# First weight sums formed in the HGRN2 stage, mixer splits one tile ahead, and a new order of the down projection's snapshots and splits

## The chip, the cores and the metric

The kernel runs on one core of one Trainium2 chip. The metric is the device time of one execution in microseconds. The kernel before has a median of 1284.31 us over three runs (1282.35 to 1285.01).

## The reference

One decoder layer for 1024 tokens of width 1024, all in fp32:

```python
u = rmsnorm(h, attn_pre_norm)
xp = u @ w_in                                  # MLA latents, rotary key, HGRN2 q, f, i, g
mix = concat(mla_mixer(...), hgrn2_mixer(...)) # 8 attention heads, 4 recurrence heads
h = h + rmsnorm(mix @ w_out, attn_post_norm)
z = rmsnorm(h, ffn_pre_norm)
ff = silu(z @ w_gate) * (z @ w_up)             # width 2816
h = h + rmsnorm(ff @ w_down, ffn_post_norm)
```

## The kernel before

Every fp32 matrix product is done as three TensorE products of values that are split in a high part (a cast on ScalarE, ACT) and a low part (a subtraction, mostly on VectorE, DVE). So each 128-row operand costs one cast and one subtraction before TensorE (PE) can use it.

The stages in order of time: the input norm with the first projection; HGRN2, a loop over four heads (L391), each with its projections and a chain of levels between PE, DVE, ACT and GpSimd (POOL); the latent projection; attention; the mixer, that is the output projection over eight row tiles of 128 tokens (L1137 to L1176) with the post norm (`post_y`, `post_z`) and the transposes into the FFN's operands (`z_t`); gate and up; down.

Both FFN matmuls use a scheme with seven products of half-size blocks in place of eight (Strassen's, in Winograd's form). It needs sums of weight blocks. For most of gate and up they are formed in the loop by DVE (`w_sums`, L1022). For the first four (block `m` = 0 to 3) `w_pre` (L1004) forms them during the mixer: two loads of 512 KB, four sums of 128x512 on POOL, two stores to the DRAM buffer `ws_d`, from where `w_load` (L996) fetches them later. Its two tiles come from the ring `wr` of two buffers (L103), which also serves the raw rows of `split`, the early weights (`w_early`, L1018) and the last row tile's input (`x_get(last)`, L927).

The mixer's tile `t` is split by `mix_load` (L826) into tiles of tags `mh` and `ml`, two buffers each; a whole tile needs both. `mix_load(t)` stands just before `mix_mm(t)` (L839), behind the norm work of tile `t - 1`. Up to L1148 a planner orders each engine's instructions by their place in the program (earlier goes first) and by when it reckons them ready, so the written place is a priority and not the final order. From L1148 on the order on each engine is the written one. Each engine runs its queue in order: an instruction that waits holds all behind it.

The down projection (L1399 to L1419) runs 77 steps: seven products of 11 steps, in the order p1, p2, p6, p5, p3, p7, p4. `d_load(n)` (L1272) fetches 512 KB for step `n` into one of four raw slots, `d_prep(n)` (L1277) splits it, five steps ahead of use, into one of eight split buffers, `d_mm(n, j)` runs its products for row block `j`. At the end of a product the last three steps (eight for p4) run block by block, and `d_post(p, j)` (L1363) reads block `j`'s result from PSUM: a copy or a sum ("snapshot"). p2 goes on accumulating in p1's banks, p3 in p5's, p7 in p6's, so that their first matmul of a block waits for that block's snapshot. p4 takes the banks that p7 has left.

Of the kernel before, what the change touches and what calls it, by code (L numbers as in the profile page):

```python
# [21 lines left out]
P = 128  # L22
S = 1024
D = 1024
# [64 lines left out]
def hymba_block(ctx: ExitStack, tc: tile.TileContext, a: dict, out: bass.AP):  # L89
# [287 lines left out]
    def chunk(x, c):  # L377
        return x[:, c * P:(c + 1) * P]

    tails = []  # L380

    def tail():
# [8 lines left out]
    for h in range(HH):  # L391
# [97 lines left out]
        for g in range(2):  # L489
            ops = sm(f"ho{h}_{g}").rearrange("p (c t) -> p c t", t=P)  # L490
            on = hp.tile([P, 4, P], F32, name=f"on{h}_{g}", tag="kn", bufs=3)
            for j in range(4):
                c = 4 * g + j
                T.matmul(ops[:, j, :], chunk(at, c), hv[:, c, h * P:(h + 1) * P], start=True, stop=(c == 0))
                if c > 0:
                    T.matmul(ops[:, j, :], chunk(q, c), st[:, c - 1, :], start=False, stop=True)
            i0 = h * NT + 4 * g
            for j in range(4):
                A.activation(on[:, j, :], ops[:, j, :], AF.Square, accum_out=ssh[:, i0 + j:i0 + j + 1])
            rsqrt(inh[:, i0:i0 + 4], ssh[:, i0:i0 + 4], 4, f"h{h}_{g}", 1.0 / P)  # L500
            for j in range(4):
                A.activation(on[:, j, :], ops[:, j, :], AF.Copy, scale=inh[:, i0 + j:i0 + j + 1])
            tails.append((h, g, on, sg))

    ssl = cst.tile([P, NT, 2], F32, name="ssl")
    inl = cst.tile([P, NT, 2], F32, name="inl")
# [319 lines left out]
    def mix_load(t, ks, mpool, tag, bufs):  # L826
        ts_ = slice(t * P, (t + 1) * P)
        for i in range(0, len(ks), 4):
            kn = ks[i:i + 4]
            k0, n = kn[0], len(kn)  # L830
            src = (mixb if k0 >= 4 else mixa)[:, k0 % 4:k0 % 4 + n, ts_]
            mh, ml = (mpool.tile([P, 4, P], F32R, name=f"m{x_}{t}_{k0}", tag=f"{tag}{x_}", bufs=bufs)[:, 0:n, :]
                      for x_ in "hl")
            A.copy(mh, src)
            V.tensor_tensor(ml, src, f32(mh), op=ALU.subtract)
            for j, k in enumerate(kn):
                mx_[t, k] = (mh[:, j, :], ml[:, j, :])

    def mix_mm(t, ks, ds=(0, 1)):  # L839
        if t not in yp_:  # L840
            if t not in Y_SMALL:
                y = big(f"y{t}")
                yp_[t] = [y[:, d_] for d_ in halves]
            else:
                yp_[t] = [sm(f"y{t}_{d}") for d in range(2)]
        for k, d in [(k, d) for k in ks for d in ds]:
            d_ = halves[d]
            mm3(yp_[t][d], mx_[t, k][0], mx_[t, k][1], wo[k][0][:, d_], wo[k][1][:, d_], k == order[0], k == order[-1])
# [138 lines left out]
            z_t2(t, tp)  # L987
            z_split("b22", tp[1], zc(t))

    w_of = {0: a["w_gate"], 1: a["w_up"]}  # L990
    seq = [(0, "p1"), (1, "p1"), (0, "p2"), (2, "p1"), (1, "p2"), (2, "p2"), (3, "p1"), (0, "p6"), (3, "p2"), (1, "p6")]
    seq += [(m, p) for p in ("p5", "p7", "p3", "p4") for m in range(2)]
    seq += [(m, p) for m in range(2, 2 * NP) for p in PRODUCTS if m > 3 or p not in ("p1", "p2")]
# [2 lines left out]
    def w_load(m):  # L996
# [3 lines left out]
        if m < PRE:  # L1000
            SP.dma_start(ffq["s1", m % 2], w_of[m % 2][m // 2 + NP][:, 512:1024])
        ws_[m] = wq.rearrange("p j (k c) -> p (j k) c", c=512)

    def w_pre(m):  # L1004
        pre_ = [wr.tile([P, D], F32, name=f"wp{m}_{j}", tag="wr") for j in range(2)]
        for j in range(2):
            SP.dma_start(pre_[j], w_of[m % 2][m // 2 + NP * j])
        (a11, a12), (a21, a22) = ([x_[:, d_] for d_ in halves] for x_ in pre_)
        G.tensor_tensor(a22, a21, a22, op=ALU.add)
        G.tensor_tensor(a21, a11, a21, op=ALU.subtract)  # L1010
        G.tensor_tensor(a11, a22, a11, op=ALU.subtract)
        G.tensor_tensor(a12, a12, a11, op=ALU.subtract)
        for j in range(2):
            SP.dma_start(ws_d[m, j], pre_[j])

    early = {}

# [110 lines left out]
    SP.dma_start(apost, a["attn_post"].partition_broadcast(P))  # L1128
    SP.dma_start(fpre, a["ffn_pre"].partition_broadcast(P))
    for t in range(NT - 1):  # L1130
        if t < 2:
            mix_load(t, order[6:8], cp, "m", 2)
            mix_mm(t, order[6:8])
        else:
            mix_load(t, order, cp, "m", 2)
            mix_mm(t, order)
        if t == 1:  # L1137
            finish_t(HEADS // 2 - 1, (1,))
        if t >= Z_LAG:
            z_t(t - Z_LAG, sm)  # L1140
        post_y(t)
        post_z(t)
        if t < PRE:
            w_pre(t)

    last = NT - 1
    mix_load(last, order, cp, "m", 2)
    ms = tc.manual_schedule(engines=None)  # L1148
    ms.__enter__()
    for x_ in "ab":  # L1150
# [121 lines left out]
    def d_load(n):  # L1272
        p, i = steps[n]
        SP.dma_start(dgen[:, n % 4, 0:512], fa_d[p][i])
        SP.dma_start(dgen[:, n % 4, 512:1024], b_src[p](i))
# [49 lines left out]
    def d_hl(n):  # L1325
        return dhp.tile([P, 2, 1024], F32R, name=f"dhl{n}", tag="dhl", bufs=8)
# [36 lines left out]
    def d_post(p, j):  # L1363
        o = dq[dbank[p]][j]
        p1, u2, u3, p5 = (x_[:, j, :] for x_ in (p1_, u2_, u3_, p5_))
        if p == "p1":
            A.copy(p1, o)  # L1367
        elif p == "p2":
            half(j, 0, o, True)
        elif p == "p6":  # L1370
            V.tensor_tensor(u2, o, p1, op=ALU.add)
        elif p == "p5":
            A.copy(p5, o)
        elif p == "p3":
            V.tensor_tensor(u2, o, u2, op=ALU.add)
            todo.append(lambda: half(j, 1, u2, False))
            todo.append(lambda: out_t(j, (0, 1), False))
        elif p == "p7":
            V.tensor_tensor(u3, o, p1, op=ALU.add)

            def c22():
                V.tensor_tensor(p5, p5, u3, op=ALU.add)
                half(4 + j, 1, p5, True)
            todo.append(c22)
        elif p == "p4":
            V.tensor_tensor(u3, o, u3, op=ALU.add)
            half(4 + j, 0, u3, False)
            out_t(4 + j, (1, 0), j == 3)
# [10 lines left out]
    for n, (p, i) in enumerate(steps):  # L1399
        if n + DN_AHEAD < len(steps):  # L1400
            if n + DN_AHEAD >= DN_EARLY + 4:
                d_load(n + DN_AHEAD)
            d_prep(n + DN_AHEAD, d_hl(n + DN_AHEAD))
        if i == 0 and p not in ("p2", "p7", "p3"):
            dq[dbank[p]] = [psd.tile([P, 512], F32, name=f"dy_{dbank[p]}{j}", tag="dy", bufs=8) for j in range(4)]
        if (p, i) in (("p4", 0), ("p3", 0)):
            for j in range(4):
                h1_load(4 * (p == "p4") + j)
        if todo and (i % 2 == 0 if p == DN_PRODUCTS[-1] else i < 8):
            todo.pop(0)()  # L1410
        tail_n = DN_END if p == DN_PRODUCTS[-1] else DN_LAST
        if i < NP - tail_n:
            for j in range(4):
                d_mm(n, j)
        elif i == NP - 1:
            for j in range(4):
                for x_ in range(n - tail_n + 1, n + 1):
                    d_mm(x_, j)
                d_post(p, j)  # L1419
    ms.__exit__(None, None, None)  # L1420
    d_st.close()
    w4_st.close()
# [87 lines left out]
```

## Time and profile before

The profiled execution took 1285.21 us; its span, from the first to the last instruction, is 1283.4 us, so 1.8 us lie around it. It is 0.9 us above the median of the three timed runs.

| engine | busy us | share of the span |
|---|---|---|
| PE (matmul) | 1230.8 | 96% |
| PEld (weight load) | 1024.2 | 80% |
| DVE | 905.6 | 71% |
| ACT | 560.4 | 44% |
| POOL | 328.5 | 26% |

A row of the timeline is start, duration, engine, line, operation, output <- inputs, shapes, count; in square brackets how long the engine had been idle just before, and what ended that. The DMA queue of the SP engine is SPq. Windows give the busy time of each engine in a stretch.

### The profile page before, as it was taken

The numbers are of one execution on the slowest core, as the hardware profiler recorded it, in microseconds if no ns is written. First come the engines' busy times: TensorE is split into PE (matmuls) and PEld (weight loads), VectorE is DVE, ScalarE is ACT, GpSimd is POOL, SyncE is SP. The second block draws the span as 40 slices with busy tenths as digits, with TensorE's granted clock in tenths as the row PEclk, the third lists the DMA queues.
The fourth block names the chain that finished last, engine by engine and source line by source line (L and its number), as shares of the span: only waits on it lengthen the run. The fifth ranks groups of instructions, "written<-read, shape, count | busy, mean of one in ns | idle before, by whom it ended". The sixth has DMA issues, their size and how long they took to land.

```text
span 1283.4 us, 18152 instructions
## 1 busy us (share of the span) xinstructions
PE 1230.8 (96%) x6436; PEld 1024.2 (80%) x6436; DVE 905.6 (71%) x1790; ACT 560.4 (44%) x1206; POOL 328.5 (26%) x395
## 2 busy tenths in 40 slices
PE   7999999999899998999999999999999998999997
PEld 6987777899788877777777888888888876888885
DVE  6836666552888889686987777767777865554586
ACT  6434343435867667443543232233232233444442
POOL 1015434321132334133003243323233432000010
PEclk8999999999999999999999999999999999999998
DMA  7240100102000002465524435444435558657691
GB/s 276 103 131 18 50 14 23 36 1 69 13 14 7 21 14 62 136 213 201 194 82 156 168 144 189 158 154 146 170 128 189 188 186 281 213 180 250 209 311 66
DMA packets 64554, 165.69 MB, mean 129 GB/s; under 512 B 7504, under 2 KB 8912, under 8 KB 64464
## 3 DMA queue, kind: packets, MB, share of 16 engines
q1 hardware_dynamic: 63360, 160.87, 36.5%
q0 software_dynamic: 1104, 3.67, 0.9%
q8 instruction: 51, 0.84, 0.3%
q14 instruction: 39, 0.32, 0.1%
HBM read 119.16 MB, written 45.35 MB: 128 GB/s over the span
## 4 chain that ended last, share of the span: by engine, by line
PE 69%; DVE 13%; DMA 6%; ACT 5%; issue 3%; POOL 3%; SPq 0%; DVEq 0%; ACTq 0%; POOLq 0%
PE g_B L1065 9%; PE g_E L1065 8%; PE g_A L1065 8%; PE dy_B L1396 5%; PE dy_E L1396 5%; PE g_C L1065 4%; PE dy_A L1396 2%; PE ao L772 2%; PE lv L441 2%; PE dy_C L1396 1%; DVE s L741 1%; PE lat_ps L99 1%; PE lat_ps L97 1%; PE lat_ps L98 1%; DMA w<-in_w_down_dram 1%
## 5 line engine op out<-in xcount | busy, mean ns | idle before, releaser
L1280 DVE TENSOR_TENSOR dhl<-w,dhl 128x1024 fp32r<-128x1024 f32 x74 | 92.3, 1267 | 65.0 <-ACT dhl L1279 64.7
L1279 ACT CAST dhl<-w 128x1024 fp32r<-128x1024 f32 x74 | 76.2, 1048 | 100.7 <-DMA w<-in_w_down_dram 29.7
L1046 ACT CAST wva<-w 128x512 fp32r<-128x512 f32 x62 | 37.8, 617 | 92.6 <-DVE w L1027 41.3
L1047 DVE TENSOR_TENSOR wva<-w,wva 128x512 fp32r<-128x512 f32 x62 | 55.5, 895 | 31.5 <-ACT wva L1046 31.3
L1046 ACT CAST wvb<-w 128x512 fp32r<-128x512 f32 x62 | 37.5, 616 | 90.4 <-DVE w L1027 49.7
L1047 DVE TENSOR_TENSOR wvb<-w,wvb 128x512 fp32r<-128x512 f32 x62 | 52.2, 843 | 32.9 <-ACT wvb L1046 32.8
L1119 POOL TENSOR_TENSOR wdr<-wdr 128x512 f32<-128x512 f32 x11 | 16.4, 1488 | 198.2 <-DMA wdr<-in_w_down_dram 184.7
L742 ACT ACTIVATE pe<-s,nm 128x128 f32<-128x128 f32 (+3 forms) x64 | 47.7, 746 | 40.3 <-DVE nm L741 24.5
L1396 PE MATMUL dy_B<-dhl 128*128 128x512 f32 x264 | 60.2, 389 | 0.0
L1396 PE MATMUL dy_E<-dhl 128*128 128x512 f32 x264 | 60.0, 389 | 0.0
L1396 PE MATMUL dy_A<-dhl 128*128 128x512 f32 x228 | 54.4, 399 | 3.9 <-ACT d_p L1367 3.1
L1396 PEld LDWEIGHTS dy_B<-dhl 128*128 128x128 f32 x264 | 49.5, 188 | 10.3
L1396 PEld LDWEIGHTS dy_E<-dhl 128*128 128x128 f32 x264 | 49.5, 188 | 10.3
L1396 PEld LDWEIGHTS dy_A<-dhl 128*128 128x128 f32 x228 | 43.7, 193 | 14.5 <-ACT d_p L1367 3.5
L763 DVE TENSOR_TENSOR ptl<-pt,pth 128x512 fp32r<-128x512 f32 (+2 forms) x96 | 49.9, 551 | 4.7 <-ACT pth L762 3.9
L759 PE MATMUL pt<-cc,pe 128*128 128x128 f32 x288 | 44.9, 276 | 5.9 <-DVE oT L778 5.6
L1099 POOL TENSOR_TENSOR fq_p<-fq_u,fq_p 128x512 f32<-128x512 f32 x11 | 19.0, 1725 | 122.9 <-DVE fq_u L1090 122.9
L741 DVE CUSTOM_DVE_ANT_0 s<-mbuf,s 128x128 f32<-128x128 bf16 (+6 forms) x56 | 41.9, 748 | 6.1 <-PE s L732 5.1
L1355 POOL DMA_DIRECT2D out_dram<-ot x8 | 4.4, 548 | 162.5 <-DVE ot L1354 162.0
L762 ACT CAST pth<-pt 128x512 fp32r<-128x512 f32 (+2 forms) x96 | 43.6, 483 | 5.4 <-PE pt L759 5.3
L462 POOL TENSOR_TENSOR kk<-kk,tt 128x128 f32<-128x128 f32 (+1 forms) x88 | 40.8, 493 | 14.1 <-PE lv L457 14.1
L759 PEld LDWEIGHTS pt<-cc,pe 128*128 128x128 f32 x288 | 34.0, 141 | 11.9 <-DVE oT L778 7.2
(478 smaller groups left out, 3886.3 us busy)
## 6 DMA issues: line engine op xcount, KB each, us to landing
w<-fa_p SPq DMA_DIRECT2D x77, 256.0 KB, 3.8
fa_p<-fq_u SPq DMA_DIRECT2D x44, 256.0 KB, 4.6
wdr<-in_w_down_dram SPq DMA_DIRECT2D x22, 512.0 KB, 6.3
wb_d<-wdr SPq DMA_DIRECT2D x22, 512.0 KB, 2.6
w<-wb_d SPq DMA_DIRECT2D x44, 256.0 KB, 3.8
w<-in_w_gate_dram SPq DMA_DIRECT2D x18, 512.0 KB, 4.8
w<-in_w_up_dram SPq DMA_DIRECT2D x18, 512.0 KB, 4.5
w<-in_w_down_dram SPq DMA_DIRECT2D x33, 256.0 KB, 4.9
```

The source lines that it names most:

```text
L462: E_.tensor_tensor(v_, v_, pick(tg, 2 * n * j + to_, t_[c_:]), op=ALU.mult)
L741: V.tensor_tensor_reduce(sv, mv, sv, op0=ALU.add, op1=ALU.min, scale=1.0, scalar=3e38, accum_out=nm)
L742: A.activation(pv, sv, AF.Exp, bias=nm, scale=-1.0, accum_out=zz[:, NT * h + qb:NT * h + qb + 1])
L759: T.transpose(tps[:, j, :], pe[:, (k0 + j) * P:(k0 + j + 1) * P], ident)
L762: A.copy(th[o], tps[:, 0:n, :])
L763: V.tensor_tensor(tl[o], tps[:, 0:n, :], f32(th[o]), op=ALU.subtract)
L1046: A.copy(wh, src)
L1047: V.tensor_tensor(wl, src, f32(wh), op=ALU.subtract)
L1065: T.matmul(o, l_[:, k_], r_[:, k, :], start=first and k == 0 and i == 0, stop=k == 3 and i == 2, skip_group_check=True)
L1279: A.copy(hl[:, 0, :], raw)
L1280: V.tensor_tensor(hl[:, 1, :], raw, f32(hl[:, 0, :]), op=ALU.subtract)
L1396: T.matmul(dq[dbank[p]][j], hl[:, lh, j_], hl[:, rh, 512:1024], start=first and x_ == 0, stop=i == NP - 1 and x_ == 2, skip_group_check=True)
```

## The change

Three edits in one. `w_pre` moves in front of the HGRN2 loop (blocks 0 and 1) and behind it (2 and 3), its sums go from POOL to DVE, and its tiles come from the HGRN2 stage's own tags `f`, `kk` and `q` and no longer from `wr`. `mix_load(t + 1)` is written right behind `mix_mm(t)`. In down, `d_prep` of a product's last step is written behind that product's matmuls and snapshots; p5's snapshot becomes a DVE sum with p1 in place of an ACT copy, and p7's adds p5 from PSUM in place of a later sum from SBUF (`c22`).

```diff
+    def w_pre(m, tags):
+        pre_ = [ht(x_, f"wp{m}_{x_}") for x_ in tags]
+        for j in range(2):
+            SP.dma_start(pre_[j], w_of[m % 2][m // 2 + NP * j])
+        (a11, a12), (a21, a22) = ([x_[:, d_] for d_ in halves] for x_ in pre_)
+        V.tensor_tensor(a22, a21, a22, op=ALU.add)
+        V.tensor_tensor(a21, a11, a21, op=ALU.subtract)
+        V.tensor_tensor(a11, a22, a11, op=ALU.subtract)
+        V.tensor_tensor(a12, a12, a11, op=ALU.subtract)
+        for j in range(2):
+            SP.dma_start(ws_d[m, j], pre_[j])
+
+    w_pre(0, ("f", "kk"))
+    w_pre(1, ("q", "q"))
...
             tails.append((h, g, on, sg))
 
+    w_pre(2, ("f", "kk"))
+    w_pre(3, ("f", "kk"))
...
     for t in range(NT - 1):
-        if t < 2:
-            mix_load(t, order[6:8], cp, "m", 2)
-            mix_mm(t, order[6:8])
-        else:
-            mix_load(t, order, cp, "m", 2)
-            mix_mm(t, order)
+        if t == 0:
+            for j in range(2):
+                mix_load(j, order[6:8], cp, "m", 2)
+        mix_mm(t, order[6:8] if t < 2 else order)
+        if t > 0:
+            mix_load(t + 1, order, cp, "m", 2)
...
-        if t < PRE:
-            w_pre(t)
 
     last = NT - 1
-    mix_load(last, order, cp, "m", 2)
...
         elif p == "p5":
-            A.copy(p5, o)
+            V.tensor_tensor(p5, o, p1, op=ALU.add)
...
         elif p == "p7":
             V.tensor_tensor(u3, o, p1, op=ALU.add)
-
-            def c22():
-                V.tensor_tensor(p5, p5, u3, op=ALU.add)
-                half(4 + j, 1, p5, True)
-            todo.append(c22)
+            V.tensor_tensor(p5, o, p5, op=ALU.add)
+            todo.append(lambda: half(4 + j, 1, p5, True))
...
             if n + DN_AHEAD >= DN_EARLY + 4:
                 d_load(n + DN_AHEAD)
+        if n + DN_AHEAD < len(steps) and i < NP - 1:
             d_prep(n + DN_AHEAD, d_hl(n + DN_AHEAD))
...
                 d_post(p, j)
+            if n + DN_AHEAD < len(steps):
+                d_prep(n + DN_AHEAD, d_hl(n + DN_AHEAD))
```

## Rows read from the trace of the kernel before

**Rows 1.** The page's first part: busy time, share and instructions of each engine.
```profile
PE 1230.8 (96%) x6436; PEld 1024.2 (80%) x6436; DVE 905.6 (71%) x1790; ACT 560.4 (44%) x1206; POOL 328.5 (26%) x395
```

**Rows 2.** Windows: stretch, length, busy us per engine, granted clock, DMA share, GB/s.
```profile
45.00:61.00 16.00, 15.34 (x126) 14.93 (x125) 15.90 (x32) 3.87 (x5) 0.00 (x0) 1.00 0.00 1
61.00:100.00 39.00, 39.00 (x196) 32.85 (x195) 12.95 (x14) 14.85 (x16) 6.59 (x9) 1.00 0.34 108
255.00:270.00 15.00, 14.10 (x127) 11.76 (x127) 12.68 (x42) 7.24 (x29) 10.55 (x23) 1.00 0.01 2
540.00:626.00 86.00, 79.22 (x367) 63.92 (x366) 66.98 (x139) 35.85 (x87) 24.85 (x16) 1.00 0.57 202
```

**Rows 3.** Timeline of PE in the mixer: the four longest waits.
```profile
566.37 0.50 PE L99 MATMUL y<-woacs,ml 128*128 128x512 f32 x1 [2.66 <-DVE ml L835]
610.18 0.50 PE L97 MATMUL y<-woah,mh 128*128 128x512 f32 x1 [1.60 <-ACT mh L834]
615.29 0.50 PE L99 MATMUL y<-woacs,ml 128*128 128x512 f32 x1 [1.36 <-DVE ml L835]
619.85 0.47 PE L97 MATMUL y<-woah,mh 128*128 128x512 f32 x1 [1.11 <-DVE rr_y L139]
```

**Rows 4.** Timeline of DVE and POOL in the mixer around the first of them.
```profile
563.38 2.31 POOL L1010 TENSOR_TENSOR wp<-wp,wp 128x512 f32<-128x512 f32 x1
564.50 1.21 DVE L140 TENSOR_TENSOR rt_y<-rr_y 128x1 f32<-128x1 f32 x1
565.63 0.68 DVE L835 TENSOR_TENSOR ml<-mixa,mh 128x512 fp32r<-128x512 f32 x1
...
590.29 0.16 DVE L140 TENSOR_TENSOR rt_y<-rr_y 128x1 f32<-128x1 f32 x1
```

**Rows 5.** The chain that ended last, late in the mixer: start, us, what.
```profile
598.01 2.93 DMA ws_d<-wp
...
601.39 5.66 DMA xr<-in_x_dram
...
609.62 0.52 ACT mh L834
```

**Rows 6.** Timeline of ACT and PE where down goes from p1 to p2.
```profile
1088.08 1.04 ACT L1279 CAST dhl<-w 128x1024 fp32r<-128x1024 f32 x1 [2.87 <-DMA w<-in_w_down_dram]
1089.41 1.04 ACT L1279 CAST dhl<-w 128x1024 fp32r<-128x1024 f32 x1 [0.29 <-DMA w<-in_w_down_dram]
1090.36 2.04 ACT L1367 COPY d_p<-dy_A 128x512 f32<-128x512 f32 x4
1090.99 1.48 PE L1396 MATMUL dy_A<-dhl 128*128 128x512 f32 x3 [3.12 <-ACT d_p L1367]
```

**Rows 7.** The chain that ended last, in down: p2's and p6's matmuls.
```profile
1090.99 31.80 PE dy_A L1396 x132
1122.80 29.92 PE dy_B L1396 x132
```

**Rows 8.** Windows: the first 3 us of p2.
```profile
1091.00:1094.00 3.00, 3.00 (x8) 2.31 (x9) 1.34 (x2) 3.00 (x5) 0.00 (x0) 0.54 0.80 253
```

**Rows 9.** Timeline where down goes from p7 to p4, and p4's last splits.
```profile
1242.52 0.69 DVE L1379 TENSOR_TENSOR d_u<-dy_B,d_p 128x512 f32<-128x512 f32 x1 [1.35 <-PE dy_B L1396]
1244.25 0.69 DVE L1382 TENSOR_TENSOR d_p<-d_p,d_u 128x512 f32<-128x512 f32 x1
1256.19 0.50 PE L1396 MATMUL dy_C<-dhl 128*128 128x512 f32 x1 [0.80 <-ACT dhl L1279]
1257.45 18.68 PE L1396 MATMUL dy_C<-dhl 128*128 128x512 f32 x74 [0.76 <-DVE dhl L1280]
```

**Rows 10.** Timeline of DVE behind p5's snapshots.
```profile
1184.24 4.63 DVE L1280 TENSOR_TENSOR dhl<-w,dhl 128x1024 fp32r<-128x1024 f32 x4 [7.42 <-ACT dhl L1279]
```

**Rows 11.** Groups by line: weight sums on DVE in the FFN (busy, mean ns).
```profile
L1043 DVE TENSOR_TENSOR w<-w 128x512 f32<-128x512 f32 x18 | 12.3, 684 | 0.0
```

**Rows 12.** One line's instructions, `w_pre`'s loads (L1007): time to landing.
```profile
DMA to landing us min/median/max: 4.5/5.0/5.5
```

More of the change, by code (lines that the diff above doesn't have):

```diff
@@ L378, in chunk @@
         return x[:, c * P:(c + 1) * P]
+    w_of = {0: a["w_gate"], 1: a["w_up"]}
+    def w_pre(m, tags):
[11 more added lines that the diff above has]
+    w_pre(1, ("q", "q"))
     tails = []
@@ L988, in z_t @@
             z_split("b22", tp[1], zc(t))
-    w_of = {0: a["w_gate"], 1: a["w_up"]}
     seq = [(0, "p1"), (1, "p1"), (0, "p2"), (2, "p1"), (1, "p2"), (2, "p2"), (3, "p1"), (0, "p6"), (3, "p2"), (1, "p6")]
@@ L1002, in w_load @@
         ws_[m] = wq.rearrange("p j (k c) -> p (j k) c", c=512)
[L1004 to L1014, printed above, removed]
     early = {}
```

## Prediction

> **What bounds the kernel now.** I read the page's shares first: PE is busy for 1230.8 of 1283.4 us [rows 1]. So nothing that only makes DVE, ACT or POOL shorter counts; what counts is the 50 us or so in which PE stands still, and the stretches in which it runs slowly. Next I cut the span into windows by stage [rows 2]. In the mixer (540 to 626) PE is busy for 79.2 of 86 us, so 6.8 us are lost there, with DMA at 0.57 of its time, POOL at 24.9 us and DVE at 67.0 us. In the HGRN2 windows PE is busy all of the time or nearly so. Then I went through PE's timeline for its waits: four in the mixer, 2.66 + 1.60 + 1.36 + 1.11 = 6.7 us [rows 3], that is the whole loss of the window; one of 3.12 us between down's first two products [rows 6]; and 0.80 + 0.76 = 1.56 us inside the last product [rows 9]. Last I read the granted clock: right behind the 3.12 us wait it is 0.54 on the mean of 3 us, where 8 matmuls start [rows 8]; 0.5 is the lower level, 1.2 GHz.
>
> **Part 1, the sums leave the mixer.** Removed there: 4 x 4 sums on POOL, 8 loads and 8 stores of 512 KB, and every use of the ring `wr` by them. Two of PE's waits hang on these.
>
> The first is 2.66 us, for the low half `ml` of a split [rows 3]. The row in front of that subtraction is a DVE operation on one column, which takes 0.16 us elsewhere and 1.21 us here; it ends at 565.71, when a sum on POOL ends (563.38 + 2.31 = 565.69) [rows 4]. So DVE operations are held by POOL's sums. Without the sums this wait goes: -2.7 us.
>
> The second is 1.60 us for a high half `mh` [rows 3]. Followed back along the chain [rows 5]: ACT casts late because it waits in its queue for the norm of tile 5's rows, which waits for that tile's input `xr`, whose load was issued at 601.39, right after a store of a sum had landed (598.01 + 2.93 = 600.94). SPq sends in order: in front of the load stood an early weight load that needed a buffer of `wr`. With the ring free that load goes early, and the input too. Besides, part 2 takes the split out from behind the norm work.
>
> Added in the HGRN2 stage: 16 sums on DVE. A sum of this shape and kind takes 0.68 us there [rows 11], so 16 x 0.68 = 10.9 us of DVE time, and the same 16 transfers. DMA is nearly idle there (0.00 to 0.34 of its time [rows 2]), so they cost no bandwidth. Eight sums (blocks 0 and 1, 5.5 us) fall near 45 to 61, where DVE is full (15.90 of 16 us), or into 61 to 100, where it idles for 39 - 12.95 = 26 us [rows 2]. In the full window part of DVE's work is the rotary tables, which stand behind the sums in the program and are not needed soon, so these would give way. But PE depends on DVE for the input's splits there and loses 16 - 15.34 = 0.7 us already. The other eight follow the last head, beside the latent projection, which asks little of DVE.
>
> What the trace does not show is DVE waiting in order for a sum's load. The lower bound is 0 (all of it hidden; no gain is possible here but the 0.7 us that PE loses now), the upper one, for a single ill-placed wait, the 5.0 us that such a load takes to land [rows 12] less the slack, some 4 us. I take +1.5 us, nearer to nothing, because PE in this stage has projections to do whatever DVE does. The stores wait on SPq for the sums; queued behind them are the projection weights, which are loaded two blocks ahead. The `f`, `kk` and `q` buffers are handed on to heads 0 and 1 when the stores have landed: with sums done near 66 us and a store of 2.9 us [rows 5] that is before head 0's `q` is written at some 85 us. I put nothing down for it.
>
> **Part 2, splits one tile ahead.** No instruction is added. Each tile needs both buffers of its tag, so the first half of the next split can run once PE is through half of the tile before, and the second half at its end, one half tile (24 matmuls, some 5.5 us) before its use. Today the split stands behind the norm work in the queues; that is the third wait, 1.36 us, where `ml` of the last tile comes behind other DVE work [rows 3]. -1.6 and -1.4 us for the second and third wait. The fourth, 1.11 us, is for PSUM that DVE empties; I leave it standing, with 0 and -1.1 us as its ends. What is moved back are the norm steps of the tile just done; they feed the transposes two tiles on, about 23 us later, which covers 2 x 1.3 us of splitting. Should that cover be gone, PE would wait for a transpose instead. Sum of the mixer: **-5.6 us**, from -2.7 to -8 (the upper end lets the fourth wait and a little over 1 us at the FFN's entry go too).
>
> **Part 3, snapshots before splits.** At the end of p1 ACT's queue holds the split of step 14, that of step 15, then the four copies. Both splits wait for their weights from DMA; the copies begin at 1090.36, PE starts 0.63 us later [rows 6]. With the split of step 15 behind, the copies follow the cast of step 14 at 1088.08 + 1.04 = 1089.12, and PE starts at 1089.75 in place of 1090.99: -1.24 us. It still waits for 1.9 us, because step 14's load is late for itself. The split of step 15 slips by 2 us; PE wants it four steps of 2.7 us later.
>
> After the wait the clock is down. p2's 132 matmuls take 31.80 us, p6's 132 at full clock 29.92 [rows 7]: 1.88 us. Waits of 1.60 and 2.66 us in the mixer were followed by no such fall (1.00 in that window [rows 2]), 3.12 us was. So 1.9 us should keep the clock up: -1.9 us, with 0 as the other end.
>
> In the last product PE waits for the split of step 76, first its cast (0.80), then its subtraction (0.76) [rows 9]. DVE is the late one. Three sums of 0.69 us [rows 9] stand in front of that subtraction, one per row block, and each also holds a Square on ACT and through it the next cast. These move into p7's end, where DVE idles for 1.35 us between blocks [rows 9], so they cost nothing there; if DVE were behind by then, p4's first matmul on that bank would wait, with 0.5 us to spare at the last block (DVE done at 1242.52 + 2 x 0.69 = 1243.9, PE there at about 1244.4). Against it the split of step 70 (1.2 us) comes into the window. Net 3 x 0.69 - 1.2 = 0.9 us of DVE work, and the idle time that the chain of sum, Square and cast leaves on DVE. The last load can be issued earlier too. I get the last subtraction ready at about 1255.5, some 0.2 us after PE wants it. So -1.2 us of the 1.56, ends 0 and -1.56. Behind this wait 74 matmuls take 18.68 us [rows 9]; at p6's pace of 29.92 / 132 = 0.227 us [rows 7] it would be 16.8: the lower clock costs 1.9 us here too. -1.9, ends 0 and -1.9.
>
> p5's copies go from ACT to DVE: behind them DVE had idled for 7.42 us [rows 10], and the next user of a block comes 2 us after its end. Nothing. At the other ends of products the moved split is due four steps later: nothing.
>
> Sum of down: -1.2 - 1.9 - 1.2 - 1.9 = **-6.2 us**, from -1.2 to -6.6.
>
> **Sum.** -5.6 - 6.2 + 1.5 = -10.3 us. Against the profiled execution 1285.2 - 10.3 = 1274.9; the median lies 0.9 us lower, so the forecast is 1284.3 - 10.3 = **1274.0**.
>
> The Trainium skill speaks against the move to DVE at one place: "GPSIMD Engine Reference", section "1. Specifications", says that POOL shares its ways into SBUF with VectorE and that DVE instructions with two SBUF inputs contend with it. The held operation above agrees, with 1.21 us for 0.16. The rule makes a rival, since the moved sums have two such inputs and HGRN2 has POOL work of its own (the fourth below).
>
> **Rivals.**
> 1. The clock still falls at one of the two places in down and the last split still is late. For it: 1.9 us of waiting is left at the first, and my margin at the second is 0.2 us. Against: the clock held after 2.66 us. Lost are 1.9 + 1.2 + some 0.6: 1277.7.
> 2. The mixer's gain is given back at the FFN's entry, where PE hangs on a row of DVE and ACT steps for the last tile. For it: DVE is busy for most of that stretch. Against: the last tile's steps begin earlier as well, and DVE is rid of the held operations. Then 1274.0 + 5.6 = 1279.6.
> 3. The change does not do what it says: the written place is only a priority, and the planner may leave the splits where they are. Then only the -2.7 us of the mixer stay: 1276.9.
> 4. Contention in HGRN2: in 255 to 270 POOL works for 10.55 and DVE for 12.68 of 15 us [rows 2]. If eight sums run there and each costs or takes the 1.05 us by which an operation was held [rows 4], it is 8.4 us in place of my 1.5: 1280.9. Against: they can run after 270.
> 5. Slower: DVE's queue stops for each of the four blocks' loads, in front of work that PE waits for. Price: 4 x (5.0 us to land [rows 12] + 4 sums of 0.68 us [rows 11]) = 31 us, 1284.3 - 11.8 + 31 = 1303 in full (11.8 is the gain without my 1.5). It decides from 11.8 + 2.6 = 14.4 us, nearly half of that price. Against: 26 us of DVE idle time behind 61 us, and DMA idle in front of it.
>
> **How the numbers follow.** Forecast 0.56, rivals in order 0.16, 0.13, 0.08, 0.03, 0.04. The low end is everything at its best end, 1284.3 - 8 - 6.6 = 1269.7 with HGRN2 at 0, and 1.7 below it for the FFN's entry: 1268. The high end takes in rivals 1 to 4: 1281. About 0.2% (2.6 us) is what a measurement of this kernel can tell from no change: faster means under 1281.7. The forecast and rivals 1 to 4 are, 0.96, less 0.05 for two of them together: faster 0.91, same 0.05, slower 0.04.
>
> **What would show it.** Right: no PE wait over 1 us in the mixer and no POOL work there; p2 starting under 2 us after p1, its matmuls in about 30 us; no drop of the clock before p4's end; HGRN2 as long as before. Wrong: in HGRN2 DVE rows that wait for `wp` from DMA with PE idle behind them, larger waits at the FFN's entry, or the halved clock still behind p1.

## The result, and the profile after

The changed kernel has a median of 1269.86 us (1268.4 to 1271.41 over four runs), beside 1283.33 us (1280.52 to 1285.01) for the kernel before on the same chip. The ratio is 0.9896, with a 95% interval of 0.9878 to 0.9915: 13.3 us faster (10.9 to 15.7 by the interval), where the forecast was 10.3 us and the low end of the range 1268. The profiled execution after took 1270.91 us with a span of 1269.1 us.

The page's first part, which answers to [rows 1]:

```profile
PE 1228.9 (97%) x6436; PEld 1026.2 (81%) x6436; DVE 906.3 (71%) x1810; ACT 559.8 (44%) x1202; POOL 306.6 (24%) x379
```

PE has the same number of matmuls and is busy for 1.9 us less; the span is 14.3 us shorter. So about 12.4 us of the gain is time in which PE stood still. DVE's total has hardly moved, although 16 sums came to it: the operations that POOL used to hold are shorter (in the mixer alone DVE is busy for 62.6 us in place of 71.7).

Windows of the kernel after; the first two answer to the first two of [rows 2], the third lies inside the mixer, as the fourth of [rows 2] does, the last three are 3 us each behind PE's waits in attention. The row by itself below them is of the kernel before, behind its first wait in attention. Columns: stretch, length, busy us of PE, PEld, DVE, ACT and POOL, granted clock, DMA share, GB/s.

```profile
45.00:61.00 16.00, 15.66 (x131) 15.46 (x130) 15.47 (x35) 3.97 (x6) 0.00 (x0) 1.00 0.55 194
61.00:100.00 39.00, 39.00 (x194) 32.76 (x194) 18.18 (x19) 15.32 (x17) 7.06 (x9) 1.00 0.39 117
...
540.00:620.00 80.00, 80.00 (x377) 66.22 (x377) 60.22 (x144) 37.62 (x91) 0.00 (x0) 1.00 0.35 119
...
380.70:383.70 3.00, 2.90 (x16) 2.50 (x17) 2.99 (x7) 2.10 (x5) 0.20 (x1) 0.76 0.00 0
476.80:479.80 3.00, 2.93 (x15) 2.69 (x16) 3.00 (x8) 2.06 (x5) 0.00 (x0) 0.67 0.00 0
502.80:505.80 3.00, 2.97 (x11) 2.56 (x12) 2.94 (x7) 2.62 (x7) 0.00 (x0) 0.50 0.34 128
```

```profile
381.20:384.20 3.00, 2.93 (x18) 2.39 (x19) 3.00 (x8) 2.41 (x6) 0.37 (x2) 1.00 0.00 0
```

In the mixer PE is busy for all of 80 us, and POOL does nothing: the four waits of [rows 3] have gone, all of them. In 45 to 61 the sums run on a DVE as full as before, and PE loses 0.3 us where it lost 0.7; the rotary tables slid into 61 to 100 (DVE 18.18 for 12.95 us). The last three rows are a loss that no part of the change makes: behind its waits of 1.84, 1.62 and 3.31 us in attention PE ran at a clock below 1.00. In the kernel before, the windows behind the first and the last of these waits (1.86 and 3.32 us there) have 1.00 and 0.50.

The chain that ended last in down of the kernel after (start, us, what), which answers to [rows 6, 7]:

```profile
1075.23 4.92 DMA w<-in_w_down_dram
...
1080.25 0.04 ACT dhl L1283
...
1081.20 0.59 ACT d_p L1371
...
1081.83 30.22 PE dy_A L1397 x132
...
1231.73 30.16 PE dy_C L1397 x132
```

The copies start as soon as step 14's cast is done. p2's matmuls take 30.22 us in place of 31.80, and the last product 30.16 us with no wait in it.

The stages of all kernels, from PE's rows: the start of the last latent-projection matmul (HGRN2 lies before it), the length of the mixer (from the start of attention's last `ao` matmul to that of the last `y` matmul), p1 with p2 (first matmul in `dy_A` to first in `dy_B`) and the end (first matmul in `dy_C` to the end of the span). All in us of the profiled executions.

| kernel | HGRN2, latent | mixer | p1 and p2 | last product to end | median | ratio, 95% |
|---|---|---|---|---|---|---|
| before | 316.2 | 93.1 | 66.4 | 41.1 | 1283.3 | |
| after | 316.2 | 84.6 | 61.4 | 37.6 | 1269.9 | 0.9896 (0.9878 to 0.9915) |
| e1 down only | 314.6 | 93.7 | 61.6 | 37.3 | 1277.6 | 0.9967 (0.9952 to 0.9982) |
| e2 without down | 317.5 | 84.7 | 64.0 | 41.1 | 1274.1 | 0.9943 (0.9923 to 0.9963) |
| e3 sums moved only | 316.6 | 84.7 | 63.7 | 41.1 | 1276.8 | 0.9951 (0.9936 to 0.9967) |
| e4 splits ahead only | 316.2 | 91.4 | 63.8 | 39.6 | 1282.3 | 1.0000 (0.9985 to 1.0016) |
| e5 sums on DVE in the mixer | 315.5 | 86.2 | 63.9 | 39.5 | 1276.8 | 0.9949 (0.9928 to 0.9970) |
| e6 POOL sums, no transfers | 317.2 | 84.7 | 65.4 | 39.5 | 1289.8 | 1.0066 (1.0043 to 1.0089) |
| e7 order only | 315.9 | 92.4 | 61.9 | 42.2 | 1283.2 | 1.0005 (0.9990 to 1.0020) |
| e8 sums from PSUM only | 316.1 | 92.1 | 65.3 | 37.3 | 1280.8 | 0.9980 (0.9963 to 0.9997) |
| e9 moved sums on POOL | 321.5 | 84.7 | 64.9 | 39.4 | 1281.8 | 0.9979 (0.9963 to 0.9996) |
| e10 two edits | 316.1 | 85.9 | 61.4 | 37.4 | 1272.7 | 0.9911 (0.9891 to 0.9930) |
| e11 attention on DVE | 316.3 | 84.6 | 62.4 | 37.4 | 1267.1 | 0.9877 (0.9854 to 0.9900) |
| e12 attention on DVE, queries too | 316.4 | 84.6 | 61.5 | 37.5 | 1266.2 | 0.9861 (0.9838 to 0.9884) |

The kernel before had medians of 1282.4 to 1283.9 us beside these; a gain below is 1 less the ratio, times that median. Single executions of one kernel lie up to 10 us apart, so the stages are compared here, and the medians decide on the sum.

### The profile page after: what moved, and what is told of

It is laid out like the page before. It is cut to its first block, busy times and chain, and to the rows that moved or that the text cites. A ratio compares the mean times of both kernels' runs of the same rounds, so it can differ in the third digit from the quotient of the medians.

```text
span 1269.1 us, 18169 instructions
## 1 busy us (share of the span) xinstructions
PE 1228.9 (97%) x6436; PEld 1026.2 (81%) x6436; DVE 906.3 (71%) x1810; ACT 559.8 (44%) x1202; POOL 306.6 (24%) x379
## 4 chain that ended last, share of the span: by engine, by line
PE 79%; DVE 9%; ACT 4%; DMA 3%; issue 2%; POOL 2%; SPq 0%; DVEq 0%; ACTq 0%; POOLq 0%
PE g_B L1072 9%; PE g_E L1072 9%; PE g_A L1072 8%; PE dy_B L1397 5%; PE dy_E L1397 5%; PE g_C L1072 4%; PE dy_A L1397 2%; PE dy_C L1397 2%; PE y L99 2%; PE y L97 2%; PE ao L792 2%; PE y L98 2%; PE lv L458 2%; PE pt L779 1%; PE lat_ps L99 1%
## 5 line engine op out<-in xcount | busy, mean ns | idle before, releaser
L1283 ACT CAST dhl<-w 128x1024 fp32r<-128x1024 f32 x74 | 76.8, 1048 | 105.1 <-DMA w<-in_w_down_dram 30.8
L1054 DVE TENSOR_TENSOR wva<-w,wva 128x512 fp32r<-128x512 f32 x62 | 56.8, 915 | 31.6 <-ACT wva L1053 31.3
L1053 ACT CAST wva<-w 128x512 fp32r<-128x512 f32 x62 | 37.7, 617 | 92.4 <-DVE w L1034 41.2
L1053 ACT CAST wvb<-w 128x512 fp32r<-128x512 f32 x62 | 37.5, 616 | 90.4 <-DVE w L1034 49.7
L1397 PEld LDWEIGHTS dy_E<-dhl 128*128 128x128 f32 x264 | 49.5, 188 | 10.3
L1397 PEld LDWEIGHTS dy_B<-dhl 128*128 128x128 f32 x264 | 49.5, 188 | 10.3
L1397 PEld LDWEIGHTS dy_A<-dhl 128*128 128x128 f32 x228 | 42.6, 188 | 10.6 <-DVE dhl L1284 1.1
```

The costliest lines, as they stand in the source:

```text
L1053: A.copy(wh, src)
L1054: V.tensor_tensor(wl, src, f32(wh), op=ALU.subtract)
L1283: A.copy(hl[:, 0, :], raw)
L1397: T.matmul(dq[dbank[p]][j], hl[:, lh, j_], hl[:, rh, 512:1024], start=first and x_ == 0, stop=i == NP - 1 and x_ == 2, skip_group_check=True)
```

## The experiments

### The parts by themselves: e1 to e4

The theory on trial was the one of the prediction: each part earns its own time in its own stage. Its rivals were luck with the clock and a transfer, a gain that is given back, and parts that depend on each other.

**e1**, down's edit alone:

```diff
+        if n + DN_AHEAD < len(steps) and i < NP - 1:
             d_prep(n + DN_AHEAD, d_hl(n + DN_AHEAD))
...
                 d_post(p, j)
+            if n + DN_AHEAD < len(steps):
+                d_prep(n + DN_AHEAD, d_hl(n + DN_AHEAD))
...
-            A.copy(p5, o)
+            V.tensor_tensor(p5, o, p1, op=ALU.add)
```

with `c22` gone as in the change.

> The kernel before with the edit of down alone (d_prep of a product's last step behind the snapshots, and p5's and p7's sums from PSUM). Theory A, each part earns its own time in its own stage: the mixer keeps its four waits (together 6.7 us), p2 starts under 2 us after p1, p2's 132 matmuls take about 30 us, p4's last two waits are gone; 6 to 8.5 us faster than before. Rival B, the gain at the p1 to p2 change came from luck of the transfer of step 14's weights and of the clock: then a wait of 2 to 3 us and the lower clock stay there and only the last product's 2 to 3.5 us are gained. Rival C, the parts hang together (the mixer's later end moves down's loads): under 2 us gained.

Measured: 4.2 us faster (ratio 0.9967), less than the 6 to 8.5 expected. The two stages are those of the kernel after (61.6 and 37.3 us, for 61.4 and 37.6), and the mixer keeps its waits (here 3.60, 0.26, 1.35 and 1.11 us: its sum stays, its parts differ from one execution to the next). So the mechanism is theory A's; why the median gains less than the profile of before promised is seen below, under the clock.

**e2**, the change without that edit.

> The changed kernel with down as before, so only the weight sums in the HGRN2 stage and the mixer's splits one tile ahead. Theory A: the mixer loses its four waits, some 6.7 to 8.7 us less in it, HGRN2 as long as before, down with its 3.12 us wait and the lower clock behind it; 5 to 8.5 us faster. If the attention stage again takes some 3 us longer with the lower clock in it, 3 to 5.5 us. Rival B (the gain is given back at the FFN's entry, or down waits longer because it is reached earlier): under 3 us. Rival D for the transfer: if the weights of step 14 now land about 5 us after their issue, as in the changed kernel, and not 6.7 as before, then the landing there depends on when down is reached, and not on the order in down.

Measured: 7.3 us faster; mixer 84.7 us, nothing given back at the FFN's entry (1.23, 1.40, 0.73 and 0.76 us of waits there, as before). 4.2 + 7.3 = 11.5 us, beside 13.3 for the whole: the parts add up within their intervals.

**e3**, only the weight sums moved, the splits where they were:

```diff
+    w_pre(0, ("f", "kk"))
+    w_pre(1, ("q", "q"))
...
+    w_pre(2, ("f", "kk"))
+    w_pre(3, ("f", "kk"))
...
-        if t < PRE:
-            w_pre(t)
```

> The kernel before with the four blocks' weight sums moved to the HGRN2 stage and to DVE, the mixer's splits where they were, down as before. Theory A, POOL's hold on DVE and the ring were behind the first two waits of the mixer: 2.66 + 1.60 us go, 1.36 and 1.11 us stay, 3 to 6 us faster, HGRN2 as long as before. Rival B, the place of the split is what mattered: a wait for the split of over 1 us stays at two places or more, and under 2.5 us are gained. Rival C, HGRN2 pays for the sums: its end comes 1.5 us or more later.

Measured: 6.3 us faster, a mixer of 84.7 us with PE busy throughout. All four waits of [rows 3] go, and not only the first two.

**e4**, only the splits one tile ahead.

> The kernel before with the mixer's splits written one tile ahead, the weight sums still on POOL in the mixer, down as before. Theory A: the waits of 1.60 and 1.36 us go or fall under 0.5 us, the first (2.66 us, a DVE operation held while a sum of POOL runs) stays for the most part, 1.5 to 4 us faster. Rival B, the split one tile ahead is all that counts, since half a tile of lead (5.5 us) covers a held DVE: all four waits go, 6 us or more. Rival C, the planner leaves the order as it was: within 0.7 us of before.

Measured: ratio 1.0000. The split moved, and the waits moved with it: 0.79, 2.28 and 0.79 us. The timeline around the second, with every engine in one view:

```profile
578.02 1.29 POOL L1010 TENSOR_TENSOR wp<-wp,wp 128x512 f32<-128x512 f32 x1
578.07 1.26 DVE L140 TENSOR_TENSOR rt_y<-rr_y 128x1 f32<-128x1 f32 x1
...
579.38 1.29 POOL L1011 TENSOR_TENSOR wp<-wp,wp 128x512 f32<-128x512 f32 x1
579.55 1.15 DVE L142 SCALAR_TENSOR_TENSOR rr_y<-rt_y,rr_y 128x1 f32<-128x1 f32 x1
580.73 2.39 DVE L946 SCALAR_TENSOR_TENSOR h<-h,rr_y,xr 128x1024 f32<-128x1024 f32 x1
580.76 1.28 POOL L1012 TENSOR_TENSOR wp<-wp 128x512 f32<-128x512 f32 x1
...
583.16 1.06 ACT L951 ACTIVATE xr<-h 128x1024 f32<-128x1024 f32 x1 [6.04 <-DVE h L946]
...
584.21 0.60 ACT L834 CAST mh<-mixb 128x512 fp32r<-128x512 f32 x1
...
584.87 0.50 PE L97 MATMUL y<-woah,mh 128*128 128x512 f32 x1 [2.28 <-ACT mh L834]
```

Two one-column operations take 1.26 and 1.15 us, each ending with a POOL sum, and the norm's product 2.39 us. ACT stands for 6.04 us in front of the norm of these rows, and the cast that PE needs comes behind it in ACT's queue. A longer lead does not help while everything in front of the split is slow.

### POOL's hold or the ring: e5 and e6

e3 takes two suspects away at once, POOL's work and the use of `wr` with its transfers. Two runs separate them.

**e5**, one word changed four times in the kernel before:

```diff
     def w_pre(m):
         pre_ = [wr.tile([P, D], F32, name=f"wp{m}_{j}", tag="wr") for j in range(2)]
...
-        G.tensor_tensor(a22, a21, a22, op=ALU.add)
+        V.tensor_tensor(a22, a21, a22, op=ALU.add)
```

> The kernel before with one edit: the four blocks' weight sums stay in the mixer, with their loads, stores and the ring wr, but DVE makes them and not POOL. Theory P, DVE operations held while POOL sums run are behind the mixer's waits: the waits of 2.66 and 1.60 us go, though DVE gets 16 x 0.68 = 10.9 us more work; 2 to 6 us faster. Rival R, the ring and the queue of SP are behind the later waits: 1.60 and 1.36 us stay, at most 3 us faster. Rival Q, DVE is too full for them (67 of 86 us busy, plus 11): new waits for ml, no gain or slower.

Measured: 6.5 us faster, as good as e3, with all transfers and the ring where they were. What its mixer loses is waits of 0.59 and 0.45 us (86.2 us for 84.7), though DVE has the sums to make there.

That settles the engine, but not the way in which its sums reach PE. The prediction read the wait of 1.60 us as that of a late load, `xr` of tile 5. In the kernel before, the load stands behind an early weight load that waits for the ring, and DVE idles until it has landed:

```profile
600.96 0.33 SPq L1020 DMA_DIRECT2D we<-in_w_up_dram  x1
601.39 0.44 SPq L931 DMA_DIRECT2D xr<-in_x_dram  x1
607.15 1.28 DVE L946 SCALAR_TENSOR_TENSOR h<-h,rr_y,xr 128x1024 f32<-128x1024 f32 x1 [3.21 <-DMA xr<-in_x_dram]
```

The DMA queue of SP in e5, and the same two loads in e7 below, whose mixer is that of the kernel before, POOL's sums and ring included:

```profile
595.69 0.33 SPq L1020 DMA_DIRECT2D we<-in_w_gate_dram  x1
596.50 0.33 SPq L931 DMA_DIRECT2D xr<-in_x_dram  x1
597.20 0.33 SPq L1020 DMA_DIRECT2D we<-in_w_up_dram  x1
```

```profile
603.51 0.33 SPq L1020 DMA_DIRECT2D we<-in_w_up_dram  x1
604.76 0.33 SPq L931 DMA_DIRECT2D xr<-in_x_dram  x1
```

In e5 the load now stands in front of the early weight load that waits for the ring. Counted back from the first matmul of the last row tile, the one that waited for 1.60 us, it is issued 8.8 us ahead in the kernel before, and 11.6 us ahead in e5 as in the kernel after. Four executions have the mixer of the kernel before, with POOL's sums and the ring, and in them the later waits follow that lead:

| kernel | `xr` issued ahead by | first wait (`ml`), us | waits in the last tile, us |
|---|---|---|---|
| before | 8.8 us | 2.66 | 1.60, 1.36, 1.11 |
| e1 | 8.8 us | 3.60 | 0.26, 1.35, 1.11 |
| e8 | 9.9 us | 3.50 | 0.58, 1.11 |
| e7 | 11.6 us | 4.83 | none |

So e5 takes away both, the held operations and the late load, and does not separate them. Rival R falls as it was put, since the ring and its transfers stay and both waits go; but a ring that comes free late, because POOL's sums end late, fits these rows as the way to the waits in the last tile. POOL's last sum ends 10.6 us ahead of the point at which PE wants that tile (13.7 us on DVE in e5), so no sum runs beside those waits. Only the first wait is a direct hold.

**e6**, the other half: e3 with 16 sums on POOL at the old place, from tiles in SBUF, no transfers.

```diff
         post_z(t)
+        if t < PRE:
+            scr = cp.tile([P, 512], BF16, name=f"scr{t}", tag="scr", bufs=1)
+            for x_, y_, d_ in ((woa[0], woa[1], 0), (woa[1], woa[0], 1), (woa[0], woa[0], 0), (woa[1], woa[1], 1)):
+                G.tensor_tensor(scr, f32(x_[:, 0, halves[d_]]), f32(y_[:, 1, halves[d_]]), op=ALU.add)
```

> The kernel e3 (sums moved to the HGRN2 stage) with 16 additional sums on POOL at the old place in the mixer, over two tiles that lie in SBUF, their results thrown away; no loads, no stores, nothing of the ring. The sums are extra work, the outputs are the reference's. Theory P: the held DVE operations come back, and with them 3 to 8 us of PE waits in the mixer, as in the kernel before. Rival R (ring and SP's queue): the mixer stays as short as in e3, within 1.5 us.

Measured: 1289.8 us, by the medians 13.0 us slower than e3 (by the ratios 14.8). The expected range was too low, because the sums, with no load to wait for, ran in a row at the mixer's entry instead of in four groups, and PE waited once:

```profile
530.34 1.27 POOL L1153 TENSOR_TENSOR scr<-woal,woah 128x512 bf16<-128x512 f32 x1
530.53 1.11 DVE L125 TENSOR_SCALAR ino<-ino 128x8 int32<-128x8 int32 x1
531.67 0.17 DVE L127 TENSOR_TENSOR ovt<-ino 128x8 f32<-128x8 f32 x1
531.69 1.28 POOL L1153 TENSOR_TENSOR scr<-woah 128x512 bf16<-128x512 f32 x1
531.88 1.12 DVE L128 SCALAR_TENSOR_TENSOR ovt<-ovt,ov 128x8 f32<-128x8 f32 x1
533.03 0.17 DVE L129 SCALAR_TENSOR_TENSOR ino<-ovt,ino 128x8 f32<-128x8 f32 x1
...
540.20 1.09 PE L843 MATMUL am<-cc,aon 128*128 128x128 f32 x4 [11.79 <-DVE aon L836]
```

This is the mechanism with nothing else around it. One eight-column DVE operation of 0.17 us gets in where one sum ends and the next begins; the one behind it starts beside a sum and ends 0.03 us after it. DVE does two small operations per 1.35 us, in a chain of some dozen, and PE waits for 11.79 us. So POOL's sums alone, without a transfer or the ring, are enough to make PE wait. The Trainium skill has the rule, "SBUF — State Buffer", section "Who interferes with whom": POOL and DVE have a pair of ports in common, and the one that comes first blocks the other for its whole instruction. The rows agree: the small operation that comes second ends 0.03 us behind the sum, not after its own 0.17 us.

### Down: e7 and e8

**e7**, only the place of the last split; **e8**, only the sums from PSUM (p5 + p1 at p5's end, p5 at p7's end, no `c22`).

> The kernel before with only d_prep of a product's last step behind the snapshots; p5's copies stay on ACT and p7's extra sums stay in p4. Theory A: the wait between p1 and p2 falls from 2.1 to 3.1 us to under 1.9, or to nothing; the last product keeps part of its waits (three sums of 0.69 us on DVE in front of the last split): 2 to 4.5 us faster. Rival B: the order does all, and the sums from PSUM nothing: as e1, p4's two waits gone too. Rival C: the order does nothing, the load of step 14 is what PE waits for: the wait stays over 2 us.

> The kernel before with only the sums from PSUM (p5 + p1 at p5's end, p5 added at p7's end, no later sum in p4). Theory A: the wait between p1 and p2 stays at 2 to 3 us, the last product loses at least one of its two waits (0.8 and 0.76 us): 1 to 3.5 us faster. Rival B: the last split's lateness is that of its load, so the waits stay: within 0.7 us of before.

Measured: e7 nothing (1.0005), e8 2.6 us faster (0.9980), where both together bring 4.2. PE in e7, behind p1 and in the last product:

```profile
1090.57 5.78 PE L1396 MATMUL dy_A<-dhl 128*128 128x512 f32 x24 [0.24 <-ACT d_p L1367]
...
1255.36 0.51 PE L1396 MATMUL dy_C<-dhl 128*128 128x512 f32 x1 [1.62 <-ACT dhl L1279]
1256.62 18.68 PE L1396 MATMUL dy_C<-dhl 128*128 128x512 f32 x74 [0.76 <-DVE dhl L1280]
```

and in e8:

```profile
1090.13 4.28 PE L1393 MATMUL dy_A<-dhl 128*128 128x512 f32 x11 [1.94 <-ACT d_p L1367]
...
1241.49 30.08 PE L1393 MATMUL dy_C<-dhl 128*128 128x512 f32 x132
```

The new order alone takes the wait behind p1 from 3.12 to 0.24 us, and makes p4's from 0.80 + 0.76 to 1.62 + 0.76: the split of step 70, moved behind p7, now stands in front of the late one. The PSUM sums alone clear p4 and leave the wait behind p1. By the medians, then, the order pays only together with the sums; but the intervals of e1 and e8 overlap, so the 1.6 us that it adds there are not certain. e7's own trace has 2 us less at p1 and 1.1 more at the end, which would be 1 us faster (against e2 to e5, whose clock stays up at p1, and against a p4 in which it falls); the median's interval (1.3 us faster to 2.6 slower) allows that.

### Where the moved sums go: e9 and e10

**e9**, e3 with the moved sums on POOL (`V.` to `G.` in `w_pre`).

> The kernel e3 with one edit: the 16 moved sums run on POOL, still in the HGRN2 stage. Theory P1, a POOL sum costs PE only where PE waits for DVE, and in the HGRN2 stage it does not: HGRN2 ends within 1 us of e3's (316.6), the whole as e3, 5 to 7 us faster than before. Rival P2, the hold costs wherever it is: each of 16 sums holds a DVE operation by about 1.05 us in a stage in which DVE feeds PE's first splits and POOL is part of the recurrence's chain: HGRN2 ends 3 to 12 us later, the gain is gone.

Measured: 2.7 us faster than before, where e3 gained 6.3. HGRN2 and the latent projection end at 321.5 in place of 316.6, 4.9 us later, and 4.6 of that are there at the first head's first projection (70.1 for 65.5 us):

```profile
47.32 1.59 POOL L388 TENSOR_TENSOR wp_kk<-wp_f,wp_kk 128x512 f32<-128x512 f32 x1
47.71 2.28 DVE L269 TENSOR_TENSOR ul<-xT,uh 128x1024 fp32r<-128x1024 f32 x1
...
50.05 0.45 PE L99 MATMUL hi_ps<-wbh,ul 128*128 128x256 f32 x1 [4.07 <-DVE ul L269]
```

The input's split takes 2.28 us, as it begins beside a sum and does its own work behind it; in the kernel after it takes 1.22:

```profile
46.41 1.22 DVE L269 TENSOR_TENSOR ul<-xT,uh 128x1024 fp32r<-128x1024 f32 x1
```

P2 holds where DVE feeds PE, for blocks 0 and 1, though a part of the gain is left; blocks 2 and 3, beside the latent projection, cost 0.3 us at most, and P1 holds there.

**e10**, e5 and e1 together, with no move to HGRN2 and no split ahead.

> The kernel before with two edits only: the weight sums on DVE at their old place in the mixer (as e5), and down's edit (as e1). No move to the HGRN2 stage, no split one tile ahead. Theory P: as fast as the whole change, -6.5 (e5) - 4.3 (e1) = -10.8 us, range 9 to 14 us faster. Rival: the move and the split one tile ahead earn something on top, then this is over 2 us slower than the changed kernel (under 11 us faster where that was 13.5).

Measured: 1272.7 us, 11.4 us faster. The intervals of e10 and of the whole change overlap, so the 1.9 us between them are not settled; 1.3 us of them is there in the stages, the mixer with sums in it (85.9 for 84.6 us). In these executions that is what the move to HGRN2 is worth; the split one tile ahead shows nowhere (e2 and e3: both 84.7 us).

### The same edit in attention: e11 and e12

If POOL's hold is the mechanism, attention should show it too. Timeline of DVE and POOL in the kernel after, in front of PE's wait of 1.84 us:

```profile
376.58 0.42 DVE L692 CAST kt1h<-kst 64x512 fp32r<-64x512 f32 x1
...
377.18 1.29 POOL L693 TENSOR_TENSOR kt1l<-kst,kt1h 64x512 fp32r<-64x512 f32 x1 [0.94 <-DVE kt1h L692]
...
377.30 1.45 DVE L692 CAST kt1h<-kst 64x512 fp32r<-64x512 f32 x1
```

**e11**:

```diff
-            wo[k] = split(wh, wl, a["w_out"][k], f"wo{k}", G)
+            wo[k] = split(wh, wl, a["w_out"][k], f"wo{k}", V)
...
-        G.tensor_tensor(kl, ks, f32(kh), op=ALU.subtract)
+        V.tensor_tensor(kl, ks, f32(kh), op=ALU.subtract)
```

**e12** has the queries' low halves on DVE as well.

> The changed kernel with the same edit in the attention stage: the low halves of the output weights (6 of 128x1024) and of the keys (14 of 64x512) are subtracted on DVE and not on POOL. Theory P: PE's waits of 1.84, 1.49, 1.62 and 3.31 us in attention, each behind a DVE operation that a POOL subtraction holds, go or fall under 0.8 us, and the lower clock behind them too: 4 to 9 us faster than the changed kernel, 17 to 23 us faster than before. Rival Q, DVE is too full there (51 to 56 of 60 to 64 us): 6 x 1.27 + 14 x 0.42 = 13.5 us more on DVE come back as waits for it, within 2 us of the changed kernel or slower.

> e11 and the low halves of the queries (14 more of 128x512, 0.69 us each on DVE) as well, which leaves POOL next to nothing to do in attention. Theory P: no worse than e11, up to 3 us better (the waits of 1.20 us go too). Rival Q, DVE full: 9.7 us more of work on DVE, 1 to 6 us slower than e11.

Measured: 1267.1 and 1266.2 us, 15.8 and 17.8 us faster than before by the ratios. Against the changed kernel (13.3 by the ratio) that is 2.5 and 4.5 us, with intervals that overlap: the best two kernels here, e12 by most, but neither margin is certain. In e11's trace:

```profile
377.67 0.48 DVE L692 CAST kt1h<-kst 64x512 fp32r<-64x512 f32 x1
...
378.45 0.69 DVE L693 TENSOR_TENSOR kt1l<-kst,kt1h 64x512 fp32r<-64x512 f32 x1
```

```profile
380.00:440.00 60.00, 57.19 (x382) 50.92 (x383) 53.57 (x168) 42.05 (x116) 11.27 (x26) 1.00 0.05 13
440.00:500.00 60.00, 56.26 (x365) 48.84 (x363) 55.27 (x165) 42.66 (x105) 12.54 (x28) 1.00 0.06 19
```

The waits of 1.84, 1.49, 1.62 and 3.31 us are gone, and the granted clock is 1.00 throughout; but waits of 1.03, 1.15, 0.84 and 1.68 us stand in that stage still or anew. That may be rival Q's part, with DVE now busy for 54 to 55 of 60 us in place of 51 to 52; their causes were not followed up. From the last latent matmul to the last `ao` matmul PE idles for 16.7 us in the kernel after, 16.2 in e11 and 15.2 in e12, while the stage shrinks from 218.7 to 213.5 and 213.6 us and its mean granted clock rises from 0.97 to 1.00. So the held casts are gone as expected, but the time comes back for the most part as clock and hardly as waiting: 4 to 9 us became 2.5.

### The clock behind a wait

The same wait, the same place, two kernels whose down is the same text. Windows behind p1's wait and behind p4's; first e2 (waits of 2.63 and 0.79 + 0.77 us), then e9 (2.10 and 0.80 + 0.76 us):

```profile
1085.60:1088.60 3.00, 3.00 (x13) 2.50 (x14) 1.33 (x2) 3.00 (x5) 0.00 (x0) 1.00 0.94 305
1250.50:1253.50 3.00, 3.00 (x8) 2.40 (x9) 2.68 (x6) 1.47 (x5) 0.00 (x0) 0.60 0.00 0
```

```profile
1089.80:1092.80 3.00, 3.00 (x10) 2.44 (x11) 1.34 (x2) 2.80 (x5) 0.00 (x0) 0.75 0.87 300
1256.30:1259.30 3.00, 2.98 (x13) 2.48 (x14) 2.71 (x5) 1.45 (x4) 0.00 (x0) 1.00 0.00 0
```

After the longer wait the clock stayed, after the shorter one it fell to the lower level (0.5 is 1.2 GHz) for a part of the window; at p4 it is the other way round. Of the eight profiled executions with the old order at p1, four show the fall there (before, e6, e8, e9: 0.54 to 0.75) and four do not (e2 to e5: 1.00). Of the eight with waits in p4, four show it (before, e2, e3, e7) and four do not. The price at p4 is 41.1 - 39.5 = 1.6 us by the table. Behind the mixer's first wait the clock is 1.00 in the kernel before (2.66 us) and 0.50 in e1, e7 and e8 (3.50 to 4.83 us).

## Why the prediction was right, and which of its steps were not

**What bounds the kernel**: right. The gain came out of the waits that [rows 3, 6, 9] list and the clock behind them; nothing came from less work.

**The mixer**: forecast -5.6 us, measured -8.5, just beyond the range given (-2.7 to -8). The held operations of [rows 4] were read rightly. So was the second wait, "Followed back along the chain [rows 5]": with the ring free the load goes 11.6 us ahead of its use in place of 8.8, and the wait is gone. The step that failed is part 2: it was given 1.6 and 1.4 us for the second and third wait, and the fourth was left standing. e3 removes all of them without part 2, e4 shows part 2 alone at nothing, and e7 has none of them where the load goes early. By these rows the third and fourth go with the same lateness. So the term of part 1 was mis-sized, -8.4 us in place of -2.7, and that of part 2 should have been 0. 6.7 us of it are the four waits; the other 1.7 us lie in PE's busy time and no row here says why.

**HGRN2**: forecast +1.5, measured 0.0 (316.2 in both; e3 0.4 more). The reason given was right: the tables give way, and PE has other work. Rival 4, contention, was worked out for POOL work that the stage already has; it did not come. e9 shows that it is real there with the sums on POOL, 4.9 us, in the first projections and not at 255 to 270. That agrees with the Trainium skill, "GPSIMD Engine Reference", section "1. Specifications", by which DVE instructions with two SBUF inputs contend with POOL.

**Down, p1 to p2**: forecast -1.24 with a wait of 1.9 left and -1.9 for the clock; measured a wait of nothing and 61.4 for 66.4 us. The step that failed is "step 14's load is late for itself". Its cast began 31.9 us after down's first matmul in the profiled execution of before, but 29.7 to 30.8 us after it in the other kernels here, old order or new: one execution's lateness was taken for the rule. In the old order the copies then follow the cast of step 15 (31.6 to 32.4 us in the others), which leaves waits of 1.9 to 2.6 us, and without the fall of the clock p1 and p2 take 63.7 to 64.0 us. So the order's own gain is 2.3 to 2.6 us, more than the 1.24 forecast.

**Down, the last product**: forecast -1.2 - 1.9, measured 41.1 to 37.6 = -3.5. e8 confirms the account of the three sums of 0.69 us in front of the late split, e7 that step 70's split comes into the window, though at 0.8 us and not 1.2 (p4's waits grow from 1.56 to 2.38).

**The clock**: its two terms of 1.9 us were right in kind for the profile they were read from, where the runs put them at 1.6 each (31.80 to 30.22 us at p2, 1.6 at p4), and wrong as terms of the median, since the fall comes in about half of the executions. That is likely why e1 gains 4.2 us and not 6 to 8.5. In the profile after, more time at the lower clock in attention took back some 3 us (attention's last `ao` matmul comes 2.8 us later than before); this loss too is luck of that execution: with the attention code unchanged, the stage from the last latent to the last `ao` matmul took 215.7 to 215.9 us where its mean granted clock was 0.99 (before, e4) and 218.7 to 220.0 where it was 0.97 (after, e2, e7, e9). The wrong terms lie on both sides: part 1 too small by 5.7, part 2 too large by 3.0, HGRN2 by 1.5, the clock by about half. The forecast was nearer than its steps, and that is luck: errors of both signs cancelled.

**The rivals**: 1, 2 and 3 did not come (no late last split, the same waits at the FFN's entry); 5 neither, DVE's waits for the four blocks' loads sum to 3.4 us, and PE loses 0.3 us in 45 to 61.

## What to carry over

When a tiny operation on DVE takes over a microsecond, look which POOL instruction ends at the same moment, and ask for every wait behind that stretch what the late instruction held up: the next operation, or a buffer and through it a load. Then change the engine first: one word in four lines (e5) gave what a new place and a new order were written for. One execution's list of waits is not the kernel's: the same mixer lost 4.8 to 6.8 us to between one and four waits. A lower clock behind a short wait should be priced at the share of executions in which it comes, and a late transfer seen in one execution should not be made a term of a sum.

## What the runs showed of the hardware

A POOL sum or subtraction (1.27 to 2.3 us) held DVE operations that began behind it until it ended: an operation of 0.17 us became 1.11 to 1.12 and ended with the sum, a 64x512 cast of 0.42 became 1.45 and a 128x1024 subtraction of 1.22 became 2.28, which ended 0.3 and 1.1 us behind it. A run of POOL sums leaves DVE about two small operations per 1.35 us (e6). Not every operation is held. In the kernel before, beside one sum:

```profile
596.37 1.61 POOL L1012 TENSOR_TENSOR wp<-wp 128x512 f32<-128x512 f32 x1
596.77 0.15 DVE L139 RECIPROCAL rr_z<-rt_z 128x1 f32<-128x1 f32 x1
596.95 1.05 DVE L140 TENSOR_TENSOR rt_z<-rr_z 128x1 f32<-128x1 f32 x1
```

The reciprocal, with one input, passes in 0.15 us; the product behind it, with two (`rr_z` twice), waits for the sum's end. The Trainium skill, "SBUF — State Buffer", section "Who interferes with whom", leaves out DVE instructions with a single SBUF input unless they run in a mode of two ports; of the held rows the cast at L692 and the scalar operation at L125 have one tile as input, and they were held all the same, which agrees if they ran in such a mode. For the cast the rows speak for it: it takes 0.42 us where a subtraction of the same 64x512 takes 0.69 (e11). For L125 no row tells.

The granted clock after PE's waits of 1.5 to 2.7 us was 1.00 in some executions and lower in others of the same code; after the wait of 3.3 us in attention it was 0.50 in all twelve traces that have one, and after the other waits of 3.12 to 11.79 us in these traces 0.50 to 0.54.
